# Hybrid encoder layer on one core: where the operands of its matrix products begin in a 256-byte line

## The chip, the cores and the metric

The kernel runs on one core of a Trainium2 chip. The metric is device time in microseconds (us), the median of three runs; the lowest and the highest run stand beside it. A profile belongs to one further execution, whose own time is given next to its span (from the first to the last instruction). The engines are named as in the profile: PE multiplies matrices, PEld is its loading of weights, DVE, ACT and POOL work on vectors, SP issues most transfers.

## The reference

One layer of an encoder over 512 tokens of width 1024. A combined projection feeds 2-D neighbourhood attention (16 heads of 64), a bidirectional state-space mixer in 8 groups, and two sigmoid gates. The branches are merged, projected, and followed by a squared-ReLU network of width 4096. Cut to what matters:

```
h = layer_norm(x, ln0_g, ln0_b)
proj = h @ w_in                               # q, k, v, z, x/B/C, dt, gates
ya = neighbourhood_attention(q, k, v, rpb) @ w_attn_br
ys = rms_norm((ssd_fwd + ssd_bwd + xs * d_skip) * silu(z)) @ w_ssd_br
mix = (gates[0] * ya + gates[1] * ys) @ w_o
h = layer_norm(DN_ALPHA * h + mix, ln1_g, ln1_b)
h = layer_norm(DN_ALPHA * h + square(relu(h @ w_ff1)) @ w_ff2, ln2_g, ln2_b)
```

## The kernel before

Every large product is made of three: each float32 operand is split into a high part (float32r) and a low rest, and `mm3` (L351) adds high by high, low by high and high by low into one PSUM bank. In `matmul(out, a, b)` the first operand `a` is loaded as weights (128 columns at a time) and the second, `b`, is streamed through: this text calls them the **stationary** and the **moving** operand. The profile writes them the other way round: in `ps_g<-hTh,wh_g` the moving operand hTh stands first.

Two shapes carry most of the time. In **512-column products** the moving operand has 512 columns: the normalised input (hTh and hTl, L395, channels on partitions, 512 tokens in a row) streams past weights for ps_x, ps_g, ps_q and ps_k; h1Th and h1Tl stream past w_ff1 for ps_f; for ps_v and the products with w_ff2 the weights stream and the activations are stationary. In **256-column products** the weights stream, 256 columns wide: ps_z (L781, the input stationary), ps_o (L1384, mgh and mgl stationary). The first half of four tiles of ps_f (L1361) streams 256 tokens.

The kernel is built in this order: normalisation and the eight groups of the mixer with their products (up to L1096, in an order that `Plan.order` works out from listed costs); v (L1120); attention in eight pairs of heads (L1156 on); its branch projection ps_abr (L1290); the remaining gates and the merge (L1314); ps_o with the second normalisation (L1373); the network ps_f (L1576 on). From L1103 on a scheduler of the framework orders the instructions of each engine when the program is built; the engines then follow that order strictly.

In attention a head goes through these steps: scores pss on PE (L1213), bias and maximum into the tile sc on DVE (L1218), exponentials on ACT (L1224), scaling on DVE (L1228), transposes tp_p on PE (L1239), the split into pth on ACT (L1243) and ptl on DVE (L1244), the product with v into po on PE (L1251), a copy low of half of po on ACT (L1262), and the sum into aT on DVE (L1265). There are two sc buffers and one low buffer. The projections ps_q and ps_k of later pairs, and at the end the gates ps_g, are what PE can do while a head is on DVE and ACT. ps_abr begins when ACT has split aT into aTh (L1276).

Tiles lie one behind another in a partition's memory, in pools, so a tile's first byte follows from the sizes of those ahead of it. Most sizes are multiples of 256 bytes; three small pads (gc_pad, rx_pad, ge_pad) and a few small tiles shift some of the others.

Of the kernel before, what the change touches and what calls it, by code (L numbers as in the profile page):

```python
# [72 lines left out]
class Plan:  # L73
# [16 lines left out]
                self.ap = self.make()  # L90
            return self.ap

    def tile(self, name, tag, pool, shape, dtype):
        return Plan.Tile(self, name, tag, lambda: pool.tile(shape, dtype, tag=tag, bufs=self.tags[tag],
                                                            name=name))

    def have(self, name, tag, ap):
        t = Plan.Tile(self, name, tag, None)
# [214 lines left out]
def encoder_layer(ctx, tc, x, w_in, w_attn_br, w_ssd_br, w_o, w_ff1, w_ff2, pcols, rows64,  # L313
# [29 lines left out]
                              op=ALU.subtract)  # L343
        return hi, lo

    def weights(parts, nk, ncol, name, eng=nc.vector, pool=None, after=None):
        hi = (pool or wp).tile([P, nk, ncol], F32R, tag="wh", name=f"wh_{name}")
        lo = (pool or wp).tile([P, nk, ncol], F32R, tag="wl", name=f"wl_{name}")
        return split_weights(parts, nk, ncol, name, hi, lo, eng, pool, after)

    def mm3(o, lh, ll, rh, rl, start, stop):  # L351
# [40 lines left out]

    hpool = tc.tile_pool(name="hT", bufs=1, reuse_waits="tile")
    xpool = hpool.__enter__()
    hTh = xpool.tile([P, KD, S], F32R, name="hTh")  # L395
    hTl = xpool.tile([P, KD, S], F32R, name="hTl")
    ysacc = xpool.tile([P, KD, S], F32, name="ysacc")

    gc = tc.tile_pool(name="gc", bufs=1, reuse_waits="tile")
    gcp = gc.__enter__()  # L400
# [51 lines left out]
    def local(name, tag, shape, dtype=F32):  # L452
        return plan.tile(name, tag, sbp, shape, dtype)

    def slab(name, parts, nk, ncol, engs):

        ws = plan.tile(f"ws_{name}", "ws", wp, [P, nk, ncol], F32)
        wh = plan.tile(f"wh_{name}", "wh", wp, [P, nk, ncol], F32R)
        wl = plan.tile(f"wl_{name}", "wl", wp, [P, nk, ncol], F32R)
# [303 lines left out]

    def group_slabs(g):
        wb = slab(f"bc{g}", [(w_in, 0, OFF_B + g * P, P), (w_in, 0, OFF_C + g * P, P)], KD, 256,
                  (nc.gpsimd, nc.gpsimd) if g else W0_ENG(nc)[:2])
        wx = slab(f"x{g}", [(w_in, 0, OFF_X + g * 256, 256)], KD, 256,
                  (nc.gpsimd, nc.gpsimd) if g else W0_ENG(nc)[2:])
        return wb, wx

    def z_project(g):
# [279 lines left out]

    def merge_gates(d2, br):

        wg = weights([(w_in, 0, OFF_G + br * D + d2 * 256, 256)], KD, 256, f"g{d2}_{br}")
        gt = gep.tile([P, 2, S], F32, tag="gt", bufs=4, name=f"gt{d2}_{br}")
        for j in range(2):
            d = 2 * d2 + j
            ps = psx.tile([P, S], F32, tag="mm", bufs=BANKS["mm"], name=f"ps_g{d}_{br}")
            project(ps, wg, j * P)
            nc.scalar.activation(gt[:, j, :], ps, AF.Sigmoid,  # L1060
                                 bias=pc[:, PC_BG + br * KD + d : PC_BG + br * KD + d + 1])
        return gt

    def gate_ops(d2, br):

        wg = slab(f"g{d2}_{br}", [(w_in, 0, OFF_G + br * D + d2 * 256, 256)], KD, 256,
                  (nc.vector, nc.vector))
# [38 lines left out]
    vpool = tc.tile_pool(name="vp", bufs=1, reuse_waits="tile")  # L1106
    vpp = vpool.__enter__()

    vhl = vpp.tile([P, 4, NH // 2, 4, HD], F32R, name="vhl")

    hb = tc.tile_pool(name="hb", bufs=1, reuse_waits="tile")
    hbp = hb.__enter__()
# [41 lines left out]
                   (s3[:, :, 0:8][:, :, ::-1], dst[:, 0, :, 0:8])])  # L1154

    for pr in range(NH // 2):  # L1156
        wqk = weights([(w_in, 0, OFF_Q + pr * P, P), (w_in, 0, OFF_K + pr * P, P)], KD, 256, f"qk{pr}")
# [4 lines left out]
        nc.scalar.activation(qf, psq, AF.Copy, scale=0.125)  # L1162
        qs = atp.tile([P, 2, 4, 8, 16], F32R, tag="qs", name=f"qs{pr}")
        halves = (slice(0, HD), slice(HD, P))
        for hh, hp in enumerate(halves):
            for sv, dv in q_views(qf[hp], qs[hp, hh]):
# [15 lines left out]
        for hh in range(2):  # L1182
# [19 lines left out]
                    in1=cst[:, CC_M0 + half * P : CC_M0 + (half + 1) * P].rearrange(  # L1202
                        "p (r j) -> p r j", r=8), op=ALU.add)
            sc = atp.tile([P, 4, 256], F32, tag="sc", bufs=2, name=f"sc{h}")
            mx = atp.tile([P, 4], F32, tag="mx", bufs=2, name=f"mx{h}")
            sums = atp.tile([P, 4], F32, tag="sums", bufs=2, name=f"sums{h}")
            for m2 in range(2):
                pss = psx.tile([P, 2, 256], F32, tag="so", bufs=BANKS["so"], name=f"pss{h}_{m2}")
# [49 lines left out]
            pv(3, 0, 1, 3, False, False)  # L1258
            pv(3, 1, 1, 0, False, True)

            low = atp.tile([P, 4, P], F32, tag="low", name=f"low{h}")
            nc.scalar.activation(low[hp], po[HD - hh * HD : P - hh * HD], AF.Copy)  # L1262
            pov, lov = (t[hp].rearrange("p m (r i) -> p m r i", r=8) for t in (po, low))
            for (dv, sv), (_, lv) in zip(q_views(aT[hp, pr, :], pov), q_views(aT[hp, pr, :], lov)):
# [30 lines left out]
    rx0 = tc.tile_pool(name="rx0", bufs=1, side="right", reuse_waits="tile")  # L1295
    rx0p = rx0.__enter__()
    rows0 = rx0p.tile([P, 2, D], F32, name="rows0")
    rx0p.tile([P, 8], F32, name="rx_pad")

    def first_norm(t, xt, eng):  # L1300

# [49 lines left out]
    w3p = ctx.enter_context(tc.tile_pool(name="w3", bufs=1, reuse_waits="tile"))  # L1351
    ep = tc.tile_pool(name="ep", bufs=1, reuse_waits="tile")
    epp = ep.__enter__()
    wo_pool = tc.tile_pool(name="wo", bufs=1, reuse_waits="tile")
    wop = wo_pool.__enter__()

# [16 lines left out]
    for t2 in range(2):  # L1373
# [15 lines left out]
        if t2:  # L1389

            early = []
            for s in range(2):
                w1 = weights([(w_ff1, 0, s * 256, 256)], KD, 256, f"f1_0_{s}")
# [21 lines left out]
    def parts(name, shape):  # L1415

        turn["parts"] += 1
        if turn["parts"] % 3 == 0:
            return third(w3p, name, shape)
        return [wp.tile(shape, F32R, tag=n, name=f"{n}_{name}") for n in ("wh", "wl")]  # L1420

    def raw(name):
        turn["raw"] += 1
# [273 lines left out]
```

## Time and profile before

| | |
|---|---|
| median of 3 runs | 1207.59 us (1206.69 to 1209.53) |
| profiled execution, own time | 1207.45 us |
| its span | 1205.7 us |
| mean granted PE clock | 0.995 of full speed |
| DVE, ACT, POOL busy | 65%, 51%, 45% of the span |
| HBM traffic | 123 GB/s over the span |
| mixer and first gates | 0 to 508 us |
| v | 508 to 552 us |
| attention | 552 to 718 us |
| branch projection, gates, merge | 718 to 807 us |
| output projection, second normalisation | 807 to 876 us |
| network | 854 us to the end |

How to read it: the duration of a product in the profile, about 389 ns for 512 columns, is its passage from start to result, and products overlap. What a product costs in a row of them is its **step**, the time from its start to the start of the next one. A window of the trace that holds nothing but one kind of product gives the step: the window's length plus one duration, divided by the count, because the count takes in the products that began just ahead of the window.

### The profile page before, as it was taken

What the parts mean: (1) busy time and instruction counts of PE and PEld (TensorE: products, weight loads), DVE (VectorE), ACT (ScalarE), POOL (GpSimd) and SP (SyncE); (2) the same over time, 40 slices, a digit from 0 to 9 for tenths busy, and PEclk for the clock granted to TensorE, in tenths of its full rate; (3) what the DMA queues carried; (4) which work ended last, traced back from release to release, by engine and by line L of the source; (5) the groups of instructions that cost most, each with busy time, mean ns of one, the idle gap of its engine ahead of it and who ended that gap; (6) DMA issues with size and microseconds to landing.
All of it is one profiled execution on the core that took longest, in us unless ns stands there. A gap on an engine that the chain in (4) does not pass through costs nothing.

```text
span 1205.7 us, 16822 instructions
## 1 busy us (share of the span) xinstructions
PE 1172.6 (97%) x6306; PEld 1004.4 (83%) x6306; DVE 780.4 (65%) x1427; ACT 608.9 (51%) x1012; POOL 541.9 (45%) x588
## 2 busy tenths in 40 slices
PE   5999999999999999999999989999999999999996
PEld 5988898989888888788888878889988888878885
DVE  7758475666666665434788975356772566398856
ACT  4576573836355563324667882342254454365410
POOL 1158977777788767303666730015153131221000
PEclk9999999999999999999999989999999999999998
DMA  7144243333333341233423323344238886778511
GB/s 231 54 144 140 88 140 105 107 117 128 105 105 112 117 138 70 71 105 89 110 60 81 84 101 109 105 145 134 72 105 207 214 202 180 189 205 216 162 49 52
DMA packets 131169, 149.21 MB, mean 124 GB/s; under 512 B 22928, under 2 KB 105488, under 8 KB 131088
## 3 DMA queue, kind: packets, MB, share of 16 engines
q1 hardware_dynamic: 118032, 113.54, 30.4%
q0 software_dynamic: 13056, 34.61, 11.8%
q8 instruction: 49, 0.80, 0.3%
q14 instruction: 32, 0.26, 0.1%
HBM read 145.90 MB, written 2.23 MB: 123 GB/s over the span
## 4 chain that ended last, share of the span: by engine, by line
PE 85%; DVE 5%; ACT 3%; DMA 3%; issue 3%; POOL 1%; SPq 0%; DVEq 0%; POOLq 0%; ACTq 0%
PE ps_f L354 8%; PE ps_f L353 8%; PE ps_f L352 8%; PE ps_x L354 5%; PE ps_x L352 5%; PE ps_x L353 5%; PE ps_z L352 3%; PE ps_z L353 3%; PE ps_z L354 3%; PE yd L932 2%; DMA w2r<-in_w_ff 2%; PE ps_sbr L352 2%; PE ps_sbr L354 2%; PE ps_sbr L353 2%; PE ps_g L352 2%
## 5 line engine op out<-in xcount | busy, mean ns | idle before, releaser
L741 DVE SCALAR_TENSOR_TENSOR cv<-ps_x,pc,cv 128x511 f32<-128x511 f32 (+1 forms) x128 | 95.8, 748 | 26.9 <-ACT cv L733 23.3
L353 PE MATMUL ps_f<-h1Th,wl_f 128*128 128x512 f32 (+1 forms) x288 | 104.7, 366 | 0.0
L352 PE MATMUL ps_f<-h1Th,wh_f 128*128 128x512 f32 (+1 forms) x288 | 104.3, 366 | 0.0
L354 PE MATMUL ps_f<-h1Tl,wh_f 128*128 128x512 f32 (+1 forms) x288 | 103.3, 367 | 1.1 <-DVE h1Tl L429 1.1
L1468 DVE TENSOR_TENSOR wl_f<-w2r,wh_f 128x1024 fp32r<-128x1024 f32 x42 | 49.8, 1220 | 64.2 <-ACT wh_f L1467 64.2
L352 PE MATMUL ps_z<-wh_z,hTh 128*128 128x256 f32 x256 | 75.9, 296 | 0.0
L354 PE MATMUL ps_z<-wl_z,hTh 128*128 128x256 f32 x256 | 72.4, 283 | 0.0
L353 PE MATMUL ps_z<-wh_z,hTl 128*128 128x256 f32 x256 | 72.3, 283 | 0.0
L1462 POOL DMA_DIRECT2D w2r<-in_w_ff x30 | 36.3, 1416 | 70.2 <-DMA w2r<-in_w_ff 46.2
L352 PE MATMUL ps_f<-wh_f,sqh 128*128 128x512 f32 x168 | 66.0, 396 | 0.7 <-ACT sqh L1467 0.7
L353 PE MATMUL ps_f<-wh_f,sql 128*128 128x512 f32 x168 | 66.2, 395 | 0.2 <-DVE sql L1468 0.2
L354 PE MATMUL ps_f<-wl_f,sqh 128*128 128x512 f32 x168 | 66.1, 395 | 0.0
L1048 DVE TENSOR_TENSOR ysacc<-ps_sbr,ysacc 128x512 f32<-128x512 f32 x56 | 38.5, 689 | 40.5 <-PE ps_sbr L354 40.3
L342 DVE TENSOR_TENSOR wl_f<-ws_f,wh_f 128x1024 fp32r<-128x1024 f32 x36 | 46.7, 1333 | 24.2 <-ACT wh_f L341 24.1
L353 PEld LDWEIGHTS ps_f<-h1Th,wl_f 128*128 128x128 f32 x288 | 54.2, 188 | 8.9
L354 PEld LDWEIGHTS ps_f<-h1Tl,wh_f 128*128 128x128 f32 x288 | 53.3, 188 | 10.0 <-DVE h1Tl L429 1.3
L352 PEld LDWEIGHTS ps_f<-h1Th,wh_f 128*128 128x128 f32 x288 | 54.1, 188 | 8.9
L1321 POOL TENSOR_TENSOR gt<-gt,ysacc 128x512 f32<-128x512 f32 x8 | 12.8, 1601 | 107.2 <-ACT gt L1060 99.1
L1467 ACT ACTIVATE wh_f<-w2r 128x1024 fp32r<-128x1024 f32 x42 | 42.5, 1052 | 34.4 <-DMA w2r<-in_w_ff 22.0
L352 PE MATMUL ps_x<-hTh,wh_bc 128*128 128x512 f32 (+1 forms) x144 | 56.9, 395 | 1.6 <-ACT wh_bc L471 1.6
L1451 POOL DMA_DIRECT2D w2r<-in_w_ff x18 | 16.1, 896 | 92.3 <-DVE wl_f L1468 55.8
L352 PE MATMUL ps_sbr<-yTh,wh_sbr 128*128 128x512 f32 x128 | 55.6, 434 | 1.2 <-DVE ysacc L1048 0.6
(327 smaller groups left out, 3900.2 us busy)
## 6 DMA issues: line engine op xcount, KB each, us to landing
ws_f<-in_w_ff SPq DMA_DIRECT2D x20, 1024.0 KB
w2r<-in_w_ff POOLq DMA_DIRECT2D x18, 1024.0 KB, 7.3
bc<-acs_d SPq DMA_DIRECT2D x32, 512.0 KB
w2r<-in_w_ff POOLq DMA_DIRECT2D x30, 512.0 KB, 8.6
ws_bc<-in_w_in SPq DMA_DIRECT2D x16, 512.0 KB
ws_x<-in_w_in SPq DMA_DIRECT2D x8, 1024.0 KB
ws_z<-in_w_in SPq DMA_DIRECT2D x8, 1024.0 KB
ws_g<-in_w_in SPq DMA_DIRECT2D x8, 1024.0 KB
```

Of the source, the lines that this page charges most:

```text
L342: (eng[i] if isinstance(eng, tuple) else eng).tensor_tensor(out=lo[:, k], in0=st[:, k], in1=hi[:, k].bitcast(F32), op=ALU.subtract)
L352: nc.tensor.matmul(o, lh, rh, start=start, stop=False)
L353: nc.tensor.matmul(o, ll, rh, start=False, stop=False)
L354: nc.tensor.matmul(o, lh, rl, start=False, stop=stop)
L741: op("DVE", 0.75, lambda j=j, o=o, n=n: nc.vector.scalar_tensor_tensor(out=acc()[:, o], in0=ps()[:, n], scalar=tap(j), in1=acc()[:, o], op ...
L932: nc.tensor.matmul(yd()[:, c % 2, h * HD : (h + 1) * HD], bc()[:, 1, h, :], xtok()[:, c, h * HD : (h + 1) * HD], start=True, stop=True)
L1048: op("DVE", 0.69, lambda d=d, ps=ps: nc.vector.tensor_tensor(out=ysacc[:, d, :], in0=ps(), in1=ysacc[:, d, :], op=ALU.add), r=[(ps.name, 0 ...
L1321: nc.gpsimd.tensor_tensor(out=g1, in0=g1, in1=ysacc[:, d, :], op=ALU.mult)
L1451: load = nc.gpsimd.dma_start(t, rows(i, n, c))
L1462: nc.gpsimd.dma_start(t, rows(i, n, c, k), accum_op=ALU.add)
L1467: nc.scalar.activation(hi[:, k], x, AF.Copy)
L1468: nc.vector.tensor_tensor(out=lo[:, k], in0=x, in1=hi[:, k].bitcast(F32), op=ALU.subtract)
```

## The change

It moves the first bytes of operands; the arithmetic stays as it is.

- The tiles wh and wl of the pool wp become 2112 words long, and a view of 2048 words in them begins at word 0 or, with `shift=16`, at byte 64. Shifted are the weights of ps_x (but for group 0), ps_g, ps_q and ps_k and the first two slabs of w_ff1.
- A pad of 64 bytes ahead of hTh moves the input to byte 64; one of 192 bytes behind ysacc restores the rest.
- qs and vhl get margins, so that they begin at byte 64; mx grows from 4 to 24 words; rx_pad and ge_pad grow, and ep_pad is new, which moves mgh, mgl, sqh, sql and one slab of w_o.
- The tile low is gone: half of po is copied into the head's own sc buffer (`low = sc[:, 0:2, :]`), which has been read by then.

The first byte modulo 256 of the two operands, with the count of float32r products, from the addresses of the two built programs:

| products, columns | count | moving, stationary before | after |
|---|---|---|---|
| ps_x, ps_g, ps_q, ps_k, 512 | 1440 | 0, 0 | 64, 64 |
| ps_f with sqh, sql, 512 | 504 | 0, 128 | 0, 0 |
| ps_f with h1T, gh; ps_sbr; ps_v; ps_abr, 512 | 1632 | 0, 0 | 0, 0 |
| ps_z, 256 | 768 | 0, 0 | 0, 64 |
| ps_f, first halves, 256 | 192 | 0, 0 | 0, 64 |
| ps_o, 256 | 288 | 0, 96 | 0, 64 |
| ps_o, one slab, 256 | 96 | 192, 96 | 0, 64 |
| ps_x of group 0 and ps_dt, 256 | 240 | 0, 0 | 64, 0 |
| pss, 256 (moving operand strided) | 128 | 0 or 64 or 128, 0 | 0 or 64 or 128, 64 |
| po, 256 and 128 | 160 | 128, 0 | 0, 64 |

```diff
+    def wide(t, nk, shift=0):
+        return t[:, shift : shift + 2048].rearrange("p (k c) -> p k c", k=nk)
-    def weights(parts, nk, ncol, name, eng=nc.vector, pool=None, after=None):
-        hi = (pool or wp).tile([P, nk, ncol], F32R, tag="wh", name=f"wh_{name}")
-        lo = (pool or wp).tile([P, nk, ncol], F32R, tag="wl", name=f"wl_{name}")
+    def weights(parts, nk, ncol, name, eng=nc.vector, pool=None, after=None, shift=0):
+        if pool:
+            hi, lo = [pool.tile([P, nk, ncol], F32R, tag=n, name=f"{n}_{name}") for n in ("wh", "wl")]
+        else:
+            hi, lo = [wide(wp.tile([P, 2112], F32R, tag=n, name=f"{n}_{name}"), nk, shift)
+                      for n in ("wh", "wl")]
...
+    xpool.tile([P, 16], F32, name="hT_pad")
     hTh = xpool.tile([P, KD, S], F32R, name="hTh")
     hTl = xpool.tile([P, KD, S], F32R, name="hTl")
     ysacc = xpool.tile([P, KD, S], F32, name="ysacc")
+    xpool.tile([P, 48], F32, name="ys_pad")
...
         wb = slab(f"bc{g}", [(w_in, 0, OFF_B + g * P, P), (w_in, 0, OFF_C + g * P, P)], KD, 256,
-                  (nc.gpsimd, nc.gpsimd) if g else W0_ENG(nc)[:2])
+                  (nc.gpsimd, nc.gpsimd) if g else W0_ENG(nc)[:2],
+                  16 if g else 0)
...
-    vhl = vpp.tile([P, 4, NH // 2, 4, HD], F32R, name="vhl")
+    vhl = vpp.tile([P, 8256], F32R, name="vhl")[:, 16:8208].rearrange(
+        "p (b r i q) -> p b r i q", b=4, r=NH // 2, i=4)
...
-        qs = atp.tile([P, 2, 4, 8, 16], F32R, tag="qs", name=f"qs{pr}")
+        qs = atp.tile([P, 1088], F32R, tag="qs", name=f"qs{pr}")[:, 16:1040].rearrange(
+            "p (h m r i) -> p h m r i", h=2, m=4, r=8)
...
-            mx = atp.tile([P, 4], F32, tag="mx", bufs=2, name=f"mx{h}")
+            mx = atp.tile([P, 24], F32, tag="mx", bufs=2, name=f"mx{h}")[:, :4]
...
-            low = atp.tile([P, 4, P], F32, tag="low", name=f"low{h}")
+            low = sc[:, 0:2, :].rearrange("p a (b i) -> p (a b) i", b=2)
...
-    rx0p.tile([P, 8], F32, name="rx_pad")
+    rx0p.tile([P, 48], F32, name="rx_pad")
...
+    epp.tile([P, 16], F32, name="ep_pad")
...
-    gep.tile([P, 24], F32, name="ge_pad")
+    gep.tile([P, 56], F32, name="ge_pad")
```

Ahead of attention, and from the branch projection on, PE, ACT and DVE keep their order. Inside it the scheduler answers to the shared buffer with another order, since the scores of head h+2 now wait until the sum of head h has been read out of the same sc buffer. The end of attention shows it on two engines. The numbers behind sc, po, pth, ps_g and so on count heads or gates.

PE before, behind the scores of the last head 15; the rows that follow are the rest of 35 gate products, with the transposes of head 14 and the product of head 13 among them:

```order
L1213 MATMUL pss15_1_6877<-kh7_6769,qs7_6721 128x256
L1214 MATMUL pss15_1_6877<-klz_4968,qs7_6721 128x256
L353 MATMUL ps_g2_1_7000<-hTh_69,wl_g1_1_6992 128x512
L354 MATMUL ps_g2_1_7000<-hTl_70,wh_g1_1_6991 128x512
L352 MATMUL ps_g2_1_7000<-hTh_69,wh_g1_1_6991 128x512
```

PE after, at the scores of head 15:

```order
L1252 MATMUL tp_p13_1_6647<-cst_83,sc13_6611 128x128 x4
L361 MATMUL ps_g3_1_7012<-hTl_71,wh_g1_1_6977 128x512
L1226 MATMUL pss15_0_6857<-kh7_6757,qs7_6709 128x256
...
L1227 MATMUL pss15_1_6864<-klz_4970,qs7_6709 128x256
L1264 MATMUL po13_6656<-pth13_0_6643,vhl_4696 128x256
```

The scores of head 15 have moved behind all gate products: no projection is left for PE between them and ps_abr, where 35 stood before.

ACT before, the last steps of attention:

```order
L1224 ACTIVATE sc15_6867,sums15_6869<-sc15_6867,mx15_6868 128x256 x4
L1243 ACTIVATE pth14_0_6822<-tp_p14_0_6817 128x512
L1262 ACTIVATE low13_6678<-po13_6667 64x512
L1243 ACTIVATE pth14_1_6831<-tp_p14_1_6826 128x512
L1060 ACT_TABLE_LOAD
L1060 ACTIVATE gt1_1_6999<-ps_g3_1_7026,pc_82 128x512
L1243 ACTIVATE pth15_0_6899<-tp_p15_0_6894 128x512
L1262 ACTIVATE low14_6846<-po14_6835 64x512
L1243 ACTIVATE pth15_1_6908<-tp_p15_1_6903 128x512
L1262 ACTIVATE low15_6923<-po15_6912 64x512
```

ACT after, from the same gate on:

```order
L1071 ACT_TABLE_LOAD
L1071 ACTIVATE gt1_1_6985<-ps_g3_1_7012,pc_84 128x512
L1275 ACTIVATE sc13_6611<-po13_6656 64x512
L1256 ACTIVATE pth14_0_6810<-tp_p14_0_6805 128x512
L1256 ACTIVATE pth14_1_6819<-tp_p14_1_6814 128x512
L1275 ACTIVATE sc14_6778<-po14_6823 64x512
L1237 ACT_TABLE_LOAD
L1237 ACTIVATE sc15_6854,sums15_6856<-sc15_6854,mx15_6855 128x256 x4
L1256 ACTIVATE pth15_0_6886<-tp_p15_0_6881 128x512
L1256 ACTIVATE pth15_1_6895<-tp_p15_1_6890 128x512
L1275 ACTIVATE sc15_6854<-po15_6899 64x512
```

The exponentials of head 15, which stood ahead of the split of head 14, now stand behind the copy of half of po14, so that heads 14 and 15 follow one another where they overlapped.

More of the change, by code (lines that the diff above doesn't have):

```diff
@@ L91, in __call__, with tile @@
             return self.ap
-    def tile(self, name, tag, pool, shape, dtype):
-        return Plan.Tile(self, name, tag, lambda: pool.tile(shape, dtype, tag=tag, bufs=self.tags[tag],
-                                                            name=name))
+    def tile(self, name, tag, pool, shape, dtype, view=lambda t: t):
+        return Plan.Tile(self, name, tag, lambda: view(pool.tile(
+            shape, dtype, tag=tag, bufs=self.tags[tag], name=name)))
     def have(self, name, tag, ap):
@@ L453, in local, with slab @@
         return plan.tile(name, tag, sbp, shape, dtype)
-    def slab(name, parts, nk, ncol, engs):
+    def slab(name, parts, nk, ncol, engs, shift=0):
         ws = plan.tile(f"ws_{name}", "ws", wp, [P, nk, ncol], F32)
-        wh = plan.tile(f"wh_{name}", "wh", wp, [P, nk, ncol], F32R)
-        wl = plan.tile(f"wl_{name}", "wl", wp, [P, nk, ncol], F32R)
+        wh, wl = [plan.tile(f"{n}_{name}", n, wp, [P, 2112], F32R, lambda t: wide(t, nk, shift))
+                  for n in ("wh", "wl")]
         c = 0
@@ L765, in group_slabs @@
         wb = slab(f"bc{g}", [(w_in, 0, OFF_B + g * P, P), (w_in, 0, OFF_C + g * P, P)], KD, 256,
-                  (nc.gpsimd, nc.gpsimd) if g else W0_ENG(nc)[:2])
+                  (nc.gpsimd, nc.gpsimd) if g else W0_ENG(nc)[:2],
+                  16 if g else 0)
         wx = slab(f"x{g}", [(w_in, 0, OFF_X + g * 256, 256)], KD, 256,
-                  (nc.gpsimd, nc.gpsimd) if g else W0_ENG(nc)[2:])
+                  (nc.gpsimd, nc.gpsimd) if g else W0_ENG(nc)[2:],
+                  16 if g else 0)
         return wb, wx
@@ L1052, in merge_gates @@
     def merge_gates(d2, br):
-        wg = weights([(w_in, 0, OFF_G + br * D + d2 * 256, 256)], KD, 256, f"g{d2}_{br}")
+        wg = weights([(w_in, 0, OFF_G + br * D + d2 * 256, 256)], KD, 256, f"g{d2}_{br}", shift=16)
         gt = gep.tile([P, 2, S], F32, tag="gt", bufs=4, name=f"gt{d2}_{br}")
@@ L1066, in gate_ops @@
         wg = slab(f"g{d2}_{br}", [(w_in, 0, OFF_G + br * D + d2 * 256, 256)], KD, 256,
-                  (nc.vector, nc.vector))
+                  (nc.vector, nc.vector), 16)
         gt = plan.tile(f"gt{d2}_{br}", "gt", gep, [P, 2, S], F32)
@@ L1156, in encoder_layer @@
     for pr in range(NH // 2):
-        wqk = weights([(w_in, 0, OFF_Q + pr * P, P), (w_in, 0, OFF_K + pr * P, P)], KD, 256, f"qk{pr}")
+        wqk = weights([(w_in, 0, OFF_Q + pr * P, P), (w_in, 0, OFF_K + pr * P, P)], KD, 256, f"qk{pr}", shift=16)
         psq = psx.tile([P, S], F32, tag="mm", bufs=BANKS["mm"], name=f"ps_q{pr}")
@@ L1392, in encoder_layer @@
             for s in range(2):
-                w1 = weights([(w_ff1, 0, s * 256, 256)], KD, 256, f"f1_0_{s}")
+                w1 = weights([(w_ff1, 0, s * 256, 256)], KD, 256, f"f1_0_{s}", shift=16)
                 for j in range(2):
@@ L1419, in parts @@
             return third(w3p, name, shape)
-        return [wp.tile(shape, F32R, tag=n, name=f"{n}_{name}") for n in ("wh", "wl")]
+        return [wide(wp.tile([P, 2112], F32R, tag=n, name=f"{n}_{name}"), shape[1])
+                for n in ("wh", "wl")]
     def raw(name):
```

## The prediction

> **What bounds the kernel now.** I read the page first, for the busy shares and the chain that ended last.
>
> ```profile
> PE 1172.6 (97%) x6306; PEld 1004.4 (83%) x6306; DVE 780.4 (65%) x1427; ACT 608.9 (51%) x1012; POOL 541.9 (45%) x588
> PE 85%; DVE 5%; ACT 3%; DMA 3%; issue 3%; POOL 1%; SPq 0%; DVEq 0%; POOLq 0%; ACTq 0%
> ```
>
> PE is the bound: busy in 97% of the span and 85% of the chain. A change in the step of its products therefore reaches the end almost whole, except where PE waits anyway. Next come windows of the trace that hold one kind of product: ps_g, ps_o with its moving operand at byte 0, ps_o with the slab at byte 192, and ps_z twice.
>
> ```profile
> core 0: us, PE busy (x), PEclk, DMA share, GB/s
> 764.00:806.00 42.00, 42.00 (x187) 1.00 0.35 111
> 807.00:836.00 29.00, 29.00 (x248) 1.00 0.46 155
> 838.00:840.50 2.50, 2.50 (x23) 1.00 0.07 18
> 52.00:62.00 10.00, 10.00 (x86) 1.00 0.56 164
> 113.00:120.00 7.00, 7.00 (x60) 1.00 0.28 92
> ```
>
> A duration is 0.39 us for 512 columns and 0.28 for 256, so the steps are 42.39/187 = 226.7 ns for ps_g (both operands at byte 0), 29.28/248 = 118.1 for ps_o (moving 0, stationary 96), 2.78/23 = 120.9 for the slab (192, 96), and 10.28/86 = 119.5 and 7.28/60 = 121.3, some 120 together, for ps_z (0, 0). The full clock is granted in all of them. The products with sqh and sql have their stationary operand at byte 128; one stretch of them, from its first start to the next other product:
>
> ```profile
> L352 PE MATMUL ps_f<-wh_f,sqh x24: 390/393/404, 946.4 to 962.4; 128*128 128x512 f32 x24
> 946.39 0.40 PE L352 MATMUL ps_f<-wh_f,sqh 128*128 128x512 f32 x1
> 963.13 0.40 PE L352 MATMUL ps_f<-h1Th,wh_f 128*128 128x512 f32 x1
> ```
>
> 24 rounds of three take 963.13 - 946.39 = 16.74 us, a step of 232.5 ns. So the same shape costs 5.8 ns more at (0, 128) than at (0, 0), without a wait. That an operand's first byte counts, by some 2%, is what this trace shows; no row stands at the pairs that the change makes.
>
> The Trainium skill says otherwise. "TensorE: Matmul & The Clock Gate", section "Step-by-step: what each phase is for", gives PE two independent read ports, one for the streamed operand and one for the weights, and its section "Back-to-back issue gap" a warm gap of N/2.4 + 2.5 ns, which is 215.8 for 512 columns and 109.2 for 256. By that no first byte would matter, and the sum would hold the order of attention alone (the second rival). The rows above lie 11 ns over both figures and differ by byte, so the trace speaks against it.
>
> **The change part by part.** The counts come from these groups, one of the three products of each:
>
> ```profile
> L352 PE MATMUL ps_f<-wh_f,sqh 128*128 128x512 f32 x168 | 66.0, 396 | 0.7 <-ACT sqh L1467 0.7
> L352 PE MATMUL ps_z<-wh_z,hTh 128*128 128x256 f32 x256 | 75.9, 296 | 0.0
> L352 PE MATMUL ps_o<-wh_o,mgh 128*128 128x256 f32 x128 | 35.7, 282 | 0.0
> L352 PE MATMUL ps_x<-hTh,wh_bc 128*128 128x512 f32 x112 | 46.9, 419 | 0.0
> L352 PE MATMUL ps_x<-hTh,wh_x 128*128 128x512 f32 x112 | 45.6, 407 | 0.0
> L352 PE MATMUL ps_g<-hTh,wh_g 128*128 128x512 f32 x128 | 50.5, 395 | 0.0
> L352 PE MATMUL ps_q<-hTh,wh_qk 128*128 128x512 f32 x64 | 25.6, 400 | 0.8 <-ACT qf L1162 0.8
> L352 PE MATMUL ps_k<-hTh,wh_qk 128*128 128x512 f32 x64 | 25.2, 394 | 0.0
> L353 PE MATMUL ps_f<-h1Th,wl_f 128*128 128x256 f32 x64 | 17.4, 284 | 0.0
> L353 PE MATMUL ps_f<-h1Th,wl_f 128*128 128x512 f32 x224 | 87.2, 389 | 0.0
> ```
>
> *sqh and sql to byte 0.* 3 x 168 = 504 products go from 232.5 to 226.7, the step that ps_g has at (0, 0): 504 x 5.8 ns = -2.9 us. PE does not wait in that stage, so all of it counts. At worst the extra comes from something else in the stage, and it is 0.
>
> *256 columns at (0, 64).* ps_z has 768 products at 120, the first halves of ps_f 192 (I give them ps_z's step), ps_o 288 at 118.1 and 96 at 120.9. The nearest row is (0, 96), 118.1; the worst is 120.9. The lower bound is the step at which only the loading of 128 weight columns is left, in the transposes:
>
> ```profile
> 401.70 1.04 PE L833 MATMUL tp_x<-cst,cv 128*128 128x128 f32 x8
> ```
>
> (1.04 - 0.27)/7 = 110 ns, with the duration of 0.27. I take 115, the middle of 110 and 120, three ns under the nearest row: ps_o at byte 96 already lies under ps_z, and byte 64 lies on that side. That is 960 x 5 + 288 x 3.1 + 96 x 5.9 ns = -6.3 us. The ends are 110 (960 x 10 + 288 x 8.1 + 96 x 10.9 = -13.0) and 120.9 (960 x 0.9 + 288 x 2.8 = +1.7).
>
> *512 columns at (64, 64).* ps_x, ps_g, ps_q and ps_k are 3 x (112 + 112 + 128 + 64 + 64) = 1440 products. No row shows the pair. The two operands keep their distance, 0, and in the rows it is the distance that sets (0, 128) apart from (0, 0); I take 0. Upper end: what sqh pays, 1440 x 5.8 = +8.4 us. Lower end: two halves at the 110 above, 220 instead of 226.7, which is -9.6.
>
> *The rest.* ps_x of group 0 and ps_dt at (64, 0), pss and po are some 500 products, at most 2 ns either way by the spread of the 256-column rows, 1 us: 0. Splits, copies and transfers keep their number and size; DVE at 65% and ACT at 51% have room, and no row shows them to depend on a first byte. Inside attention SP issues four weight loads one head's bias rows earlier or later, which the two buffers of each slab cover: 0.
>
> *The shared sc buffer.* This adds a wait: the scores of head h+2 behind the sum of head h. What counts is PE's idle time, since its work stays the same.
>
> ```profile
> core 0: us, PE busy (x) PEld busy (x) DVE busy (x) ACT busy (x) POOL busy (x), PEclk, DMA share, GB/s
> 552.00:700.00 148.00, 146.55 (x821) 126.14 (x820) 121.06 (x343) 104.09 (x281) 96.40 (x159) 1.00 0.33 79
> 700.00:718.00 18.00, 14.83 (x81) 12.06 (x79) 11.38 (x42) 13.68 (x28) 5.14 (x7) 0.91 0.18 61
> ```
>
> Up to 700 us PE idles 1.5 us, so there is little to win. At the end the order has no projection left behind the scores of head 15, and head 15 follows head 14. The rows of before with which I build the new end:
>
> ```profile
> 709.44 0.39 PE L354 MATMUL ps_g<-hTl,wh_g 128*128 128x512 f32 x1
> 718.10 0.79 PE L352 MATMUL ps_abr<-aTh,wh_abr 128*128 128x512 f32 x1 [1.38 <-ACT aTh L1276]
> 708.97 0.60 ACT L1243 ACTIVATE pth<-tp_p 128x512 fp32r<-128x512 f32 x1
> 709.59 1.28 ACT L1060 ACT_TABLE_LOAD   x1
> 710.89 0.69 ACT L1060 ACTIVATE gt<-ps_g,pc 128x512 f32<-128x512 f32 x1
> 712.75 0.59 ACT L1262 ACTIVATE low<-po 64x512 f32<-64x512 f32 x1 [0.69 <-ACT pth L1243]
> 707.26 0.50 ACT L1224 ACTIVATE sc<-sc,mx 128x256 f32<-128x256 f32 x1
> 709.87 0.99 DVE L1265 TENSOR_TENSOR aT<-po,low 64x128 f32<-64x128 f32 x5
> 709.15 0.69 DVE L1244 TENSOR_TENSOR ptl<-tp_p,pth 128x512 fp32r<-128x512 f32 x1
> 708.10 1.15 DVE L1228 TENSOR_SCALAR sc<-sc,sums 128x256 f32<-128x256 f32 x4
> ```
>
> Before, the last gate product ends its step at 709.67 and ps_abr begins 8.4 us later; two halves of transposes and two po are 3.1 us of steps in it, so PE idles 5.3. Now, from the end of that product: pth13 0.6, table 1.3 and gate 0.7, copy of po13 0.6, sum 1.0, two ptl14 1.4, po14 done 1.0 later, copy 0.7, table 1.3, four exponentials 2.0, reciprocal 0.35, scaling 1.15, transposes 0.5, two pth15 1.2, ptl15 0.7, po15 1.2, copy 0.7, aTh 0.65: 17.0 us. PE's work in it is 6.0 (scores, three po, four halves of transposes, by 110 to 120 ns each): 11.0 idle, 5.7 more than before. Less part of the 1.5 from the earlier heads: **+5**. Ends: +2, if a table load and a copy lie beside DVE's steps; +9, if the clock, granted at 0.91 in the last row but one above all because PE idles there, falls longer.
>
> **The sum**, against the profiled execution's own 1207.45 us (span 1205.7, and 1.75 around it; the median is 1207.59): -2.9 - 6.3 + 0 + 5 = -4.2, that is **1203.2 us**.
>
> **The rivals.**
>
> 1. *The shifted pair pays (slower).* If PE wants the moving operand at byte 0 of 256 and it is not the distance that counts, the 1440 products of the input pay up to 5.8 ns: 1203.2 + 8.4 = 1211.6. From 2.9 ns a product it eats the gain. For it: every row at 226.7 has the moving operand at byte 0, and the slab at 192 costs 2.8 ns more than that at 0. Against it: there the distance differs too. 0.13.
> 2. *The bytes do nothing, the order costs (slower).* Then sqh's 5.8 ns belong to its stage, and only the end of attention is left: 1207.45 + 5 = 1212.4. The page of the Trainium skill named above would have it so. Against it: h1T's products in the same stage stay at 389 ns by their group, sqh's are at 396. 0.07.
> 3. *Byte 64 is like byte 96 and attention takes what it gives.* 256 columns at 118.1: 960 x 1.9 + 96 x 2.8 = -2.1, sqh -2.9, attention +6: 1208.5, from 1205 to 1210. For it: the row is the nearest there is. 0.22.
> 4. *More than I take.* At 110 ns, or with ps_x, ps_g, ps_q and ps_k a few ns down as well: 1207.45 - 2.9 - 13 + 5 = 1196.5, from 1190 to 1200. For it: 226.7 and 120 both lie some 10 ns above what two independent streams would need by the 110 ns row. 0.18.
>
> **How the numbers follow.** The forecast, 1200 to 1206.5, has 0.40. A measurement of this kernel tells 0.2% from no change, some 2.4 us. Faster than 1205.2: 0.36 of the forecast, 0.18 of the fourth and 0.01 of the third: 0.55. Within 0.2%: 0.04 of the forecast, 0.14 of the third, 0.03 of the first: 0.21. Slower: 0.10, 0.07 and 0.07: 0.24. The range, 1193 to 1212, leaves out the far ends of the fourth and of the two slower cases.
>
> **What would show it.** A window of ps_f with sqh at 226.7 ns shows the first term; ps_z and ps_o near 115 the second (118 speaks for the third rival, 110 for the fourth); ps_g still at 226.7 the third, and 229 or more the first rival. Attention is right if PE idles about 11 us between the last gate product and ps_abr, and little before. Wrong would be the prediction if heads in the middle of attention now wait as well, or if steps move that have kept their bytes (ps_v, ps_sbr, ps_f with h1T).

## The result, and the profile after

The changed kernel takes 1236.97 us (median of 6 runs, 1234.25 to 1239.31) where the kernel before took 1208.45 (6 runs, 1206.69 to 1212.47): a ratio of 1.0233, 95% interval 1.0212 to 1.0253. It is slower by some 28 us. The profiled execution of it took 1238.38 us, with a span of 1236.6. The prediction had the other sign.

The page of the changed kernel, its busy times, its chain that ended last, and the granted clock in 40 slices of the span:

```profile
PE 1182.5 (96%) x6306; PEld 1011.8 (82%) x6306; DVE 775.1 (63%) x1427; ACT 609.6 (49%) x1012; POOL 542.6 (44%) x588
PE 85%; DVE 6%; DMA 3%; ACT 3%; issue 2%; POOL 1%; DVEq 0%; ACTq 0%; POOLq 0%
PEclk9999999999999999999998887999999999999998
```

The two shares of PE, 96% and 85%, are almost those of before: a page over the whole span hides what happened. The clock row shows the place, the four slices from 649 to 773 us. So the next view is the windows, cut at the first product of a stage: mixer, attention and network, first of the kernel before, then of the changed one.

```profile
0.00:509.00 509.00, 492.42 (x2859) 428.42 (x2859) 324.48 (x561) 286.07 (x430) 347.14 (x357) 1.00 0.36 117
552.60:718.10 165.50, 160.78 (x897) 137.72 (x896) 132.54 (x386) 117.84 (x307) 101.54 (x165) 0.99 0.32 78
854.00:1205.70 351.70, 339.90 (x1579) 281.72 (x1577) 225.41 (x329) 146.37 (x198) 67.14 (x55) 0.99 0.58 156
```

```profile
0.00:509.50 509.50, 491.30 (x2859) 425.97 (x2859) 322.73 (x561) 286.21 (x430) 346.36 (x357) 1.00 0.37 117
553.12:751.07 197.95, 174.59 (x897) 147.49 (x895) 129.25 (x386) 117.06 (x306) 102.83 (x165) 0.91 0.26 65
887.00:1236.60 349.60, 337.01 (x1579) 281.78 (x1577) 225.43 (x329) 146.39 (x198) 67.19 (x55) 0.99 0.59 157
```

The first number behind the window is its length. Attention grew from 165.5 to 197.95 us, +32.4; the rest of the span gave back 1.5, the network 2.1 of it. In attention PE has the same 897 products in both. Its idle time there, the length less its busy time, grew from 4.7 to 23.4 us, and its busy time from 160.8 to 174.6, at a granted clock (third number from the end) of 0.91. What PE waited for inside attention, by the view of waits, before:

```profile
PE po L1251 <- DVE aT L1265: 2.0, 3, 1.3
PE ps_abr L352 <- ACT aTh L1276: 1.4, 1, 1.4
PE ps_q L352 <- ACT qf L1162: 0.8, 1, 0.8
PE po L1251 <- ACT qf L1162: 0.4, 1, 0.4
```

and after:

```profile
PE po L1265 <- DVE ptl L1257: 5.7, 4, 2.4
PE ps_g L359 <- ACT qf L1174: 5.5, 1, 5.5
PE tp_p L1252 <- DVE sc L1241: 4.8, 1, 4.8
PE po L1264 <- ACT pth L1256: 3.3, 4, 1.8
PE pss L1226 <- DVE mx L1231: 2.3, 3, 1.1
PE ps_abr L359 <- ACT aTh L1289: 1.3, 1, 1.3
```

(us in all, times, the longest.) No single wait carries it: several steps of a head are waited for, from the maximum to the split, and once the copy of a projection (qf). A chain that runs through several engines, with none of them always busy, would look like this; whether it is the bound, the next rows and the runs tell.

**The chain.** Follow head 13 on DVE. Before, its first maximum, and the first maximum of head 15, which takes the same sc buffer; the sum of head 13 stands in the prediction, at 709.87:

```profile
683.90 0.41 DVE L1218 CUSTOM_DVE_ANT_0 sc<-pss,bias 128x256 f32<-128x256 f32 x1
704.09 0.40 DVE L1218 CUSTOM_DVE_ANT_0 sc<-pss,bias 128x256 f32<-128x256 f32 x1
```

After, the same two, and between them the copy of po13 on ACT and the start of the sum:

```profile
718.56 0.41 DVE L1231 CUSTOM_DVE_ANT_0 sc<-pss,bias 128x256 f32<-128x256 f32 x1
735.06 0.59 ACT L1275 ACTIVATE sc<-po 64x512 f32<-64x512 f32 x1 [0.93 <-PE po L1265]
735.68 0.29 DVE L1278 TENSOR_TENSOR aT<-po,sc 64x128 f32<-64x128 f32 x1 [1.94 <-ACT sc L1275]
737.91 0.41 DVE L1231 CUSTOM_DVE_ANT_0 sc<-pss,bias 128x256 f32<-128x256 f32 x1
```

Before, the maximum of head 15 began 5.8 us ahead of the sum of head 13 (6.8 ahead of its end); after, 1.2 us behind its end. That holds for every head: between the end of the sum of head h and the first maximum of head h+2 lie -2.8 to -11.3 us before (14 of 14 below zero) and +0.1 to +2.3 after (14 of 14 above). What that means for the pace, from the same rows over the heads:

| | head, first maximum to end of sum, mean of heads 2 to 13 | pair of heads, first maximum of head 2 to that of head 12, over 5 | attention |
|---|---|---|---|
| before | 26.4 us (23.2 to 31.1) | 17.7 us | 165.5 us |
| after | 21.7 us (18.1 to 24.5) | 22.1 us | 198.0 us |

Before, 26.4/8.85 = three heads were under way at a time, though there are two sc buffers: a buffer was free again once the transposes had read it. Held to the sum, it allows two, and a pair can come no faster than one head takes. Heads got shorter, 21.7 us, but a pair now takes that plus the gap.

The first maximum of head 14, before and after:

```profile
695.48 0.41 DVE L1218 CUSTOM_DVE_ANT_0 sc<-pss,bias 128x256 f32<-128x256 f32 x1
```

```profile
727.19 0.42 DVE L1231 CUSTOM_DVE_ANT_0 sc<-pss,bias 128x256 f32<-128x256 f32 x1 [0.17 <-PE ps_g L361]
```

Counted from the start of attention it stands at 142.9 us before and at 174.1 after. So 31.2 of the 32.4 us are lost by then.

**The clock.** Of the 32.4 us, 18.6 are idle time of PE; the other 13.8 are busy time for the same products. Most of that is a low clock behind the waits: steps that are over 30% longer than usual, where half the clock was granted, come to 11.2 us above the usual steps after and to 0.7 before (counted from the starts in the two traces). The rest is not taken apart; a row of products that a wait cuts into shorter ones also counts the passage of a last product more often. The row of the longest wait, and two that follow it:

```profile
694.15 0.80 PE L359 MATMUL ps_g<-hTh,wh_g 128*128 128x512 f32 x1 [5.54 <-ACT qf L1174]
694.75 0.63 PE L360 MATMUL ps_g<-hTh,wl_g 128*128 128x512 f32 x1
697.30 0.41 PE L360 MATMUL ps_g<-hTh,wl_g 128*128 128x512 f32 x1
```

From 694.75 six steps take (697.30 - 694.75)/6 = 425 ns where the step is 227: the wait of 5.5 us cost another 1.5 us behind it. The granted clock is 0.50 from 690.5 to 697.3 us. The Trainium skill, "TensorE: Matmul & The Clock Gate", section "Part 1: The HAM clock gate", has half the clock as the idle state, and 426.7 ns for 512 columns at it; with 0.50 and 425 ns the trace agrees. The page puts the idle window ahead of it at about 3.4 us. Here the clock fell sooner: 1.9 us into this wait, and at 629.1 us at the end of a wait of 2.0.

### The profile page after: what moved, and what is told of

Same layout as the page of the kernel before. It is cut to its first block, busy times and chain, and to the rows that moved or that the text cites. A ratio compares the mean times of both kernels' runs of the same rounds, so it can differ in the third digit from the quotient of the medians.

```text
span 1236.6 us, 16817 instructions
## 1 busy us (share of the span) xinstructions
PE 1182.5 (96%) x6306; PEld 1011.8 (82%) x6306; DVE 775.1 (63%) x1427; ACT 609.6 (49%) x1012; POOL 542.6 (44%) x588
## 4 chain that ended last, share of the span: by engine, by line
PE 85%; DVE 6%; DMA 3%; ACT 3%; issue 2%; POOL 1%; DVEq 0%; ACTq 0%; POOLq 0%
PE ps_f L360 8%; PE ps_f L361 8%; PE ps_f L359 8%; PE ps_x L359 4%; PE ps_x L361 4%; PE ps_x L360 4%; PE ps_g L359 2%; PE ps_g L361 2%; PE ps_g L360 2%; PE ps_z L359 2%; PE ps_z L360 2%; PE yd L943 2%; PE ps_z L361 2%; DMA w2r<-in_w_ff 2%; PE ps_sbr L359 2%; PE ps_sbr L361 2%
## 5 line engine op out<-in xcount | busy, mean ns | idle before, releaser
L750 DVE SCALAR_TENSOR_TENSOR cv<-ps_x,pc,cv 128x511 f32<-128x511 f32 (+1 forms) x128 | 95.8, 749 | 26.4 <-ACT cv L742 22.9
L1477 POOL DMA_DIRECT2D w2r<-in_w_ff x30 | 36.3, 1416 | 71.0 <-DMA w2r<-in_w_ff 46.6
L1334 POOL TENSOR_TENSOR gt<-gt,ysacc 128x512 f32<-128x512 f32 x8 | 12.8, 1609 | 113.8 <-ACT gt L1071 105.7
L1482 ACT ACTIVATE wh_f<-w2r 128x1024 fp32r<-128x1024 f32 x42 | 42.5, 1052 | 35.2 <-DMA w2r<-in_w_ff 23.4
L359 PE MATMUL ps_g<-hTh,wh_g 128*128 128x512 f32 x128 | 51.5, 402 | 5.5 <-ACT qf L1174 5.5
```

Of the source, the lines that this page charges most:

```text
L359: nc.tensor.matmul(o, lh, rh, start=start, stop=False)
L750: op("DVE", 0.75, lambda j=j, o=o, n=n: nc.vector.scalar_tensor_tensor(out=acc()[:, o], in0=ps()[:, n], scalar=tap(j), in1=acc()[:, o], op ...
L1334: nc.gpsimd.tensor_tensor(out=g1, in0=g1, in1=ysacc[:, d, :], op=ALU.mult)
L1477: nc.gpsimd.dma_start(t, rows(i, n, c, k), accum_op=ALU.add)
L1482: nc.scalar.activation(hi[:, k], x, AF.Copy)
```

## The experiments

Each is timed beside the kernel before on the same chip; the difference is that of the two medians.

| run | what it is | time | ratio, 95% interval | difference |
|---|---|---|---|---|
| e1 | sharing alone | 1240.31 | 1.0285 (1.0267 to 1.0303) | +33.0 |
| e2 | all bytes, no sharing | 1204.46 | 0.9981 (0.9972 to 0.9991) | -2.8 |
| e3 | sqh and sql to byte 0 | 1206.33 | 0.9985 (0.9973 to 0.9997) | -1.0 |
| e4 | map of the bytes | 1208.44, one run | | |
| e5 | sharing, heads 12 to 15 | 1212.08 | 1.0042 (1.0028 to 1.0055) | +5.3 |
| e6 | sharing, heads 0 to 11 | 1237.08 | 1.0258 (1.0223 to 1.0293) | +30.3 |
| e7 | sharing, three buffers | 1214.44 | 1.0058 (1.0038 to 1.0078) | +7.7 |
| e8 | sharing, two by hand | 1235.92 | 1.0235 (1.0205 to 1.0265) | +29.1 |
| e9 | the copy's place alone | 1208.79 | 1.0021 (1.0008 to 1.0034) | +2.7 |
| e10 | e2 again | 1204.51 | 0.9981 (0.9971 to 0.9992) | -1.6 |
| e11 | all bytes, own low, one raw | 1214.05 | 1.0054 (1.0036 to 1.0073) | +6.2 |

### Sharing or bytes: e1 and e2

e1 is the kernel before with

```diff
-            low = atp.tile([P, 4, P], F32, tag="low", name=f"low{h}")
+            low = sc[:, 0:2, :].rearrange("p a (b i) -> p (a b) i", b=2)
```

> The kernel before with one line of the change: half of po is copied into the head's own sc buffer; every operand keeps its bytes, and the order in attention becomes that of the change. Theory A (sharing the buffer costs the time): attention grows from 165.5 us to about 198, and the time is 1208 + 32 = about 1240 us. Theory B (the new bytes of qs, vhl and mx slow attention, and sharing costs the +5 that I forecast): about 1212 us. Theory C (neither alone, both together): about 1208 to 1212 us.

e2 is the changed kernel with

```diff
-            low = sc[:, 0:2, :].rearrange("p a (b i) -> p (a b) i", b=2)
+            low = (aT[:, pr + 1].rearrange("p (m i) -> p m i", m=4) if pr + 1 < NH // 2
+                   else sc[:, 0:2, :].rearrange("p a (b i) -> p (a b) i", b=2))
```

> The changed kernel with all its bytes, but half of po is copied into a part of aT that is still unused (the columns of the next pair; the last pair, behind whose sums no scores follow, keeps the shared buffer), so the scores of head h+2 wait for nothing new, and every engine has the order of before. Theory A: attention is back at about 165.5 us, and only what lies outside it is left: mixer +0.5, network -2.1, the rest about 0, so about 1206 us (1203 to 1207). Theory B: about 1233 us, attention at 190 us or more. By my forecast's byte terms alone (-2.9 and -6.3) it would be 1198 us.

Measured: +33.0 us and -2.8 us; attention 197.7 us in e1, 167.3 in e2. Attention in e1, in the columns of the windows above:

```profile
554.86:752.54 197.68, 174.78 (x898) 146.93 (x896) 129.37 (x386) 117.18 (x306) 102.43 (x165) 0.91 0.26 65
```

Idle time, busy time and clock of PE are nearly those of the changed kernel. Sharing alone gives all of the loss, with every operand at its old byte; the bytes without it gain. The two add up to +30.2, and the change had +28.5. Theory B and C fall. The order of instructions in e1 is that of the changed kernel on all five engines, and in e2 that of before, so the four kernels make a square of two causes, but for the place of the copy in e2, which e9 prices.

### The end of attention or its whole length: e5 and e6

Both are the kernel before with the line of e1 for some heads and that of e2 for the others (`h >= 12` in e5, `h < 12` in e6):

```diff
-            low = atp.tile([P, 4, P], F32, tag="low", name=f"low{h}")
+            low = (sc[:, 0:2, :].rearrange("p a (b i) -> p (a b) i", b=2) if h >= 12 or pr == 7
+                   else aT[:, pr + 1].rearrange("p (m i) -> p m i", m=4))
```

> The kernel before, with the sharing of sc for the last four heads alone (12 to 15), so that only the scores of heads 14 and 15 wait for a sum; heads 0 to 11 copy half of po into the unused columns of aT and keep the order of before. Theory D (a buffer that is held through the whole head sets the pace: two heads can start no sooner than a head's time from its maximum to its sum, about 22 us, where before a pair took 17.8): one such step, about +4.5 us, and the end of attention, which my forecast put at +5: 1212 us, from 1210 to 1216. Theory E (the loss arises at the end of attention, where no projection is left): nearly all of the 33 us, 1230 us or more.

> The kernel before, with the sharing of sc for heads 0 to 11 alone, so that the scores of heads 2 to 13 wait and those of heads 14 and 15 do not. Theory D: six steps of 4.5 us each, +27 us, of which what is left of PE's waits at the end may take back some 5: 1229 to 1236 us. Theory E: the end of attention is as before, so 1207 to 1212 us.

Measured: +5.3 us with the last heads alone, +30.3 with the first twelve. A pair takes 17.7 us up to head 12 in e5, and 22.1 us in e6, as in the changed kernel. The loss is one of the pace, paid at each step; theory E falls. e6 came out just above its forecast of 1229 to 1236 us. The two add up to 35.6, 2.6 more than sharing for all; the intervals of the three runs are too wide to read anything into that.

### The number of buffers: e7 and e8

```diff
+    scs = [atp.tile([P, 4, 256], F32, tag=f"sc_{i}", name=f"sc_{i}") for i in range(2)]
+    scs.append(aT[:, 6:8].rearrange("p k (a c) -> p (k a) c", a=2))
...
-            sc = atp.tile([P, 4, 256], F32, tag="sc", bufs=2, name=f"sc{h}")
+            sc = scs[h % 3 if h < 12 else h % 2]
```

with the line of e1 for all heads; e8 has `h % 2` throughout.

> The kernel before, with the sharing of sc for every head, but with three sc buffers in turn for heads 0 to 11 (the third lies in the last 1024 columns of aT, which no head has written by then); heads 12 to 15 alternate between the first two. Three heads may then be under way: theory D gives a buffer three times 8.9 = 26.7 us for a head that took 23 to 31 us before, so most of the loss goes and about one step of it stays at the end: 1210 to 1218 us. If the loss comes from the order that the scheduler makes, or from the copy into sc itself, and not from the number of heads under way: 1235 us or more.

> The control of e7_three_buffers: sc shared by every head, and the same two buffers named by hand, alternating for all heads. Theory D: two heads under way, so about 1240 us as in e1_share_alone, though the order differs from it in places. If naming the buffers by hand changes more than their number: away from 1240 by over 6 us.

Measured: +7.7 us with three buffers, +29.1 with two. A pair takes 18.4 us in e7, with heads of 27.2; 21.5 in e8. With a third buffer the same sharing, the same copy into sc and the same late release cost a quarter: the number of heads under way is what counts. e8 lies 4 us under e1. There the maxima of the scores that go to the half of sc without the copy run ahead of the sum, so the buffer is held by halves; by how much that and the other order each help was not taken apart.

### The bytes: e3 and e4

e3 is the kernel before with

```diff
-    rx0p.tile([P, 8], F32, name="rx_pad")
+    rx0p.tile([P, 40], F32, name="rx_pad")
...
-    gep.tile([P, 24], F32, name="ge_pad")
+    gep.tile([P, 56], F32, name="ge_pad")
```

> The kernel before with ge_pad at 56 words (and rx_pad at 40, so that mgh and mgl keep byte 96): of the matrix operands only sqh and sql move, from byte 128 to byte 0. If the byte is the cause of the 232.5 ns step: the step of their 504 products falls to 226.7 to 228 ns, and the time by 2 to 3 us, to about 1205. If the extra belongs to the stage and not to the byte: the step stays at 232 ns and the time at 1208.

Measured: a step of 227 ns for the products with sqh and sql (median; 232 before), the network 348.4 us instead of 351.7. The time came down by 1.0 us between the medians and by 0.15%, some 1.8 us, by the ratio (0.4 to 3.3 by its interval), less than the 2 to 3 us expected and the 3.3 of the network; in the profiled execution the mixer, whose matrix operands the edit leaves alone, took 2 us longer than in that of before. The step shows that the byte is the cause.

e4 is e2 with the shift of the weights by group:

```diff
-                  16 if g else 0)
+                  16 * (g % 4))
...
-        wh, wl = slab(f"z{g}", [(w_in, 0, OFF_Z + g * 256, 256)], KD, 256, (nc.gpsimd, nc.gpsimd))
+        wh, wl = slab(f"z{g}", [(w_in, 0, OFF_Z + g * 256, 256)], KD, 256, (nc.gpsimd, nc.gpsimd),
+                      16 * (g % 4))
```

> The kernel of e2_bytes_alone, with the shift of the weights varied by group: the weights of group g's ps_x and ps_z begin at byte 64 x (g mod 4). With the input at byte 64 that gives (moving, stationary) = (64, 0), (64, 64), (64, 128), (64, 192) for 512 columns and (0, 64), (64, 64), (128, 64), (192, 64) for 256. If the distance of the two bytes counts: 512 columns at (64, 64) stay at 226.7 ns and (64, 192), at a distance of 128, costs some 232; for 256 columns (192, 64) is the worst and the others are lower. If the absolute bytes count: (64, 128), with the stationary operand at sqh's byte, costs some 232. If bytes count for nothing in these products, all are alike within 1 ns. The time itself says little here: about 1206 to 1212 us.

For each pair of bytes, the first of 24 products of ps_x in a row and the first product behind them, from the timeline, in the order stationary operand at 0, 64, 128, 192:

```profile
262.74 0.39 PE L359 MATMUL ps_x<-hTh,wh_bc 128*128 128x512 f32 x1
268.24 0.22 PE L944 MATMUL yd<-xtok,bc 128*128 128x64 f32 x1
318.70 0.39 PE L359 MATMUL ps_x<-hTh,wh_bc 128*128 128x512 f32 x1
324.14 0.39 PE L359 MATMUL ps_x<-hTh,wh_x 128*128 128x512 f32 x1
149.51 0.40 PE L359 MATMUL ps_x<-hTh,wh_bc 128*128 128x512 f32 x1
155.11 0.22 PE L944 MATMUL yd<-xtok,bc 128*128 128x64 f32 x1
427.74 0.47 PE L359 MATMUL ps_x<-hTh,wh_bc 128*128 128x512 f32 x1
433.41 0.40 PE L359 MATMUL ps_x<-hTh,wh_bc 128*128 128x512 f32 x1
```

Divided by 24: 229.2 ns at (64, 0), 226.7 at (64, 64), 233.3 at (64, 128), 236.3 at (64, 192). The last stretch is a slow one: its first product took 0.47 us, and over all products of ps_x the medians are 229 ns at (64, 0), 227 at (64, 64), 233.5 at (64, 128) and 232 at (64, 192), two groups of the mixer for each pair (one for (64, 0)). The same products in e2, all at (64, 64), have a median of 227 in every group, so it is not the group. The distance is 64 both at (64, 0) and at (64, 128), with 2 and 6 ns more than at (64, 64): the distance alone does not set it. A stationary operand at 128 or beyond is the dear one, here as with sqh. For 256 columns the medians are 117 ns at (0, 64), 120 at (64, 64), 118 at (128, 64) and 119 at (192, 64).

### What the bytes are worth, and a better kernel: e9, e10 and e11

e9 is the kernel before with the line of e2.

> The kernel before, all bytes as they were, with half of po copied into the unused columns of aT as in e2_bytes_alone: what that place costs by itself. In e2_bytes_alone ACT's last table load ahead of the exponentials of head 15 waited for the maximum, 1.90 us idle, where before it went ahead of it. If that belongs to the place of the copy: +1 to +2 us, 1208 to 1209 us, and the bytes of e2_bytes_alone are worth that much more than its own ratio shows, some -4 us. If it belongs to the bytes: no difference from before.

> e2_bytes_alone once more, on the chip of e9_place_alone: 1204.5 us, ratio 0.998; from e9_place_alone to this one, the bytes alone, -3 to -5 us by theory, of -6.7 us that the steps of ps_z, ps_o, the first halves of ps_f and the products with sqh and sql give.

Measured: +2.7 us for the place and -1.6 for place and bytes together, so the bytes are worth 1208.79 - 1204.51 = 4.3 us. The row of ACT's last table load ahead of the exponentials of head 15, in e2 and in the kernel before:

```profile
705.04 1.28 ACT L1237 ACT_TABLE_LOAD   x1 [1.90 <-DVE mx L1235]
```

```profile
703.92 1.28 ACT L1224 ACT_TABLE_LOAD   x1
```

In e2 it waits for the maximum, where before it was done by then; in e9, with the old bytes, it waits as long (1.91 us), so that belongs to the place of the copy. Attention is 167.1 us in e9 and 165.5 before. Where the rest of the 2.7 us lies is not shown: e2 and e10, one program, differ by 1.1 us in attention between their two profiled executions, and two mixers that are alike, before and in e1, by 2.2.

e11 is the changed kernel with its own low buffer and `bufs=1` for raw.

> The changed kernel with all its bytes and with a low buffer of its own as before; the 1 KB of a partition that this lacks comes from raw, which holds the bias rows of one head instead of two. The table load of e9_place_alone waits for nothing here. If one raw buffer is enough: the bytes alone, -4 to -5 us, 1201 to 1203 us, faster than e2_bytes_alone. If loading the bias rows late delays the maxima: attention above 168 us and the time at 1206 or more. The scheduler makes another order for it, so a loss would not tell the two reasons apart.

Measured: +6.2 us, attention 175.6 us. The table load waits for nothing there, but a single raw buffer, or the order that comes with it, costs more than the bytes gain; as expected, the run does not tell these two apart. So e2 is the best of them: 0.19% faster than before, in both of its timings, and some 2.5% faster than the change.

## Why the prediction failed, point by point

**Sharing sc, +5: the step that failed.** It measured +33.0 (e1). The step reads: "Up to 700 us PE idles 1.5 us, so there is little to win", and then builds the new end alone. A PE that hardly idles says what a change can win there, not what it can lose: it shows that the chain of a head had room, and not how much. The room was in the rows of before. A head took 26.4 us from its first maximum to the end of its sum, and a buffer came round every 17.7. Holding the buffer to the sum asks two of them for 26.4 in 17.7. What I called the wrong case, that "heads in the middle of attention now wait as well", was the likely one by that comparison. Its size could be bounded too: between no loss, if heads shrank to 17.7, and 7 steps of 26.4 - 17.7 = 8.7, some 61 us; it came out at 7 x (22.1 - 17.7) = 31, by which head 14 was late.

With sharing for the last heads alone (e5) the loss is +5.3 us, the size of my +5, but that is luck and no test of the end that I built. In e5 11 gate products still stand behind the scores of head 15, where the changed kernel has none. Its head 14 waits for the sum of head 12 and begins 4.9 us later than before, and its attention is 4.1 us longer: one step of the pace, as theory D has it, and nothing behind it.

In the changed kernel the end is longer than I built it. From the end of the last gate product's step to ps_abr before, and from the start of the last gate product, 0.2 us more, after:

```profile
709.67:718.10 8.43, 5.16 (x29) 4.07 (x29) 4.75 (x18) 4.84 (x8) 1.29 (x1) 0.81 0.02 10
726.67:751.07 24.40, 14.20 (x58) 11.19 (x56) 12.63 (x51) 13.21 (x30) 2.97 (x5) 0.60 0.01 3
```

I had 17.0 us for it, beginning with the split of head 13 on ACT. In the trace another step stands ahead of that split:

```profile
728.95 0.51 ACT L1237 ACTIVATE sc<-sc,mx 128x256 f32<-128x256 f32 x1 [4.66 <-DVE mx L1235]
730.56 0.60 ACT L1256 ACTIVATE pth<-tp_p 128x512 fp32r<-128x512 f32 x1
744.57 1.94 PE L1252 MATMUL tp_p<-cst,sc 128*128 128x128 f32 x8 [4.76 <-DVE sc L1241]
```

The exponentials of head 14, late from the middle, come first, and the split begins 3.9 us after the start of the last gate product. The clock of 0.60 adds to it: eight transposes take 1.94 us, where the prediction's row of eight has 1.04. PE is busy for 14.2 of the 24.4 us, where I had put its work at 6.0; the two are not quite the same measure, since busy time counts the passage of each row's last product and my 6.0 counts steps alone.

My sign for attention was that PE would idle about 11 us behind the last gate product "and little before". It idles 24.4 - 14.2 = 10.2 us there, but also 23.4 - 10.2 = 13.2 us before it, where it had idled 1.5. The first half came out near, in an end 7 us longer than mine; the second names what I had left out.

**sqh and sql, -2.9: right.** From the first product of a stretch of 72 to the next other product:

```profile
978.61 0.39 PE L359 MATMUL ps_f<-wh_f,sqh 128*128 128x512 f32 x1
994.93 0.39 PE L359 MATMUL ps_f<-h1Th,wh_f 128*128 128x512 f32 x1
```

16.32/72 = 226.7 ns, as forecast, and e3 moved no other matrix operand. As time, e3's interval, 0.4 to 3.3 us, holds the 2.9 but does not single it out. The second rival, that bytes do nothing, falls with it, and so does what I drew from the Trainium skill for it ("TensorE: Matmul & The Clock Gate", "Step-by-step: what each phase is for"). The page gives PE two independent ports; that no first byte would matter was my inference. Here the byte of the stationary operand alone changes the step.

**256 columns at (0, 64), -6.3: right in kind, too large.** Windows of the changed kernel, ps_o and two of ps_z:

```profile
842.00:871.00 29.00, 29.00 (x249) 29.00 (x247) 18.88 (x44) 5.77 (x7) 18.52 (x7) 1.00 0.46 146
52.00:62.00 10.00, 10.00 (x87) 10.00 (x86) 9.54 (x18) 5.57 (x7) 0.00 (x0) 1.00 0.57 167
113.00:120.00 7.00, 7.00 (x64) 7.00 (x63) 5.02 (x8) 6.64 (x11) 6.11 (x13) 1.00 0.20 83
```

By the rule of the prediction they are 29.28/249 = 117.6, 10.28/87 = 118.2 and 7.28/64 = 113.8 ns: I took 115 for all. The step at this pair has two values; ps_z and ps_o are mostly at the upper one (medians 117 and 118), the first halves of ps_f at the lower (114). Over all of them the mean step fell by 3.1 ns for ps_z, 4.9 for the first halves of ps_f, 0.1 for ps_o and 2.6 for its one slab (e2 against before, from start to start, gaps left out): 768 x 3.1 + 192 x 4.9 + 288 x 0.1 + 96 x 2.6 ns = 3.6 us. With sqh that makes some -6.5, and -4.3 was measured as time (e9 to e10). Where the other 2 us stayed is not shown; that the mixer did not pass its part on in full, since PE waits there for others as well, is a guess.

**512 columns at (64, 64), 0: right in value, wrong in reason.** e4 has 226.7 ns there, so the first rival's price was not paid. But "it is the distance that sets (0, 128) apart" does not hold, by the rows of e4.

**The other rivals.** The third, byte 64 like byte 96 with attention eating the gain, was nearest in its steps (118 of ps_o; its 2.1 us against my 6.3, where 3.6 came out) and far off in its time, since it put attention at +6. The fourth leaned on a reading that was off: by the row of 110 ns, 512 columns lie 6.7 ns above two streams, as my own lower end of 220 says, and not some 10. The range failed with the forecast: all five cases took attention from the same one step.

## What to carry to other kernels

Before you let a tile live longer, read how long its contents would have to stand, from first write to last read, and compare it with the number of buffers times the pace at which they come round; an engine that is busy all the time says nothing about that, since it is the very overlap that is taken away. Where the hold is longer than that product, reckon the difference once per round, over the whole stage and not only at its end. That is an upper bound, because the hold can shorten when fewer are under way: here 4.4 of 8.7 us a round were paid. A place whose next use is far off (here the columns of the next pair) costs far less than one whose next use is waiting.

## What the runs showed of the hardware

- The step of a product with 512 columns depends on the stationary operand's first byte modulo 256: with the moving operand at byte 64, medians of 227 ns at 64, 229 at 0, 233.5 at 128 and 232 at 192 (e4); with the moving one at 0 it was 226.7 at 0 and 232.5 at 128 (before; 232 and 227 for the same products in before and e3).
- With 256 columns, (0, 64) gave 113.8 and 118.2 ns in different tiles of one run, at the same bytes. The first 96 products of ps_z had a median step of 113 ns in e2 and of 118 in e10, which are one program. So neither the bytes nor the program sets the two apart, and no run here says what does.
- Behind a wait of 5.5 us, PE took one step of 600 ns and six of 425 before the step was near 227 again; the granted clock had halved 1.9 us into the wait. In attention steps at half the clock cost 10.5 of the 32.4 us lost.
- ACT's table load waited for the maximum in e2 and e9 and went ahead of it in the kernel before, at the same place in the order: 1.9 us of idle time on ACT, with nothing changed in e9 but where the copy is kept. Why the place of the copy does this, no run shows.
